# Squares of the attention heads summed during the attention, and an output phase without GpSimd whose blocks end one block later

## The chip, the cores and the metric

The kernel runs on one core of one Trainium2 chip. A core has TensorE (PE: matmuls, and PEld, their weight loads), VectorE (DVE), ScalarE (ACT), GpSimd (POOL), SyncE (SP, which issues transfers here), 16 DMA engines, the on-chip memory SBUF and the matmul accumulators in PSUM. The metric is the device time of one execution in microseconds, as the median of several.

## The reference, cut to what matters

One layer of a hybrid encoder over 4096 new tokens and 32 sample tokens, width 1024. A projection feeds a group of four differential-attention heads (values of 128) and a pooling group; both are gated, joined, multiplied by an output matrix, added to the residual, and normalised. The part that the change touches is the path from a head's output to the layer's output:

```
o = diff_attention(q, k, v)                       # per token and head: 128 values
o = rmsnorm(o, subln_g, 1e-5) * (1.0 - lam_init)  # root of the mean square of each head
a_out = o * silu(ga)
p_out = pool_mix(u) * silu(gp)
y = x + concat(a_out, p_out) @ w_out
y_out = rmsnorm(y, final_g, 1e-6)
```

## The kernel before

Work is cut into 32 blocks of 128 tokens and one block of 32 (the sample). Matmuls that need full precision are done as three products of a high and a low half (`mm3`, lines 112 to 114). Four phases follow one another on PE: the projection (`token_phase`), the gates and the pooling (`channel_phase`), the attention (`attention_phase`), and the output (`output_phase`).

The attention goes row by row; a row is one head and one block of queries, 128 rows in all. A row's scores (L616) are reduced to a maximum on DVE (L513), turned into exponentials on ACT (L522), joined on DVE (L554), transposed on PE (L560), copied on ACT (L563) and multiplied with the values on PE (L644). When the last value matmul of a row is done, DVE writes `ot`, the head's output, from the accumulator `av` (L649, two buffers), and SP stores it in `o_scr` (L650). One call of `step` puts at most one tile of scores, one transpose and one value product into the program. While work lasts, `step` also puts filler matmuls in between: the remaining channel work and `PoolPart`, the pooling half of the output product (`yp`, stored in `x_scr`), of which ten units are kept for the end.

The output phase takes the blocks in the order `LAST`. `heads_in` loads a block's head outputs and its gates into one tile (`on` and `gt`, shown as og), four blocks ahead, and works out the norm: a maximum (L908), a scale for very large values, four Squares on ACT (L916), nine small DVE operations on 4 columns, a root on ACT (L922) and a product on GpSimd (L929). `mixed` transposes the four heads on PE into the one PSUM tile with the tag tp (L935), multiplies them with the gate on DVE (L936), makes the high half on ACT (L938) and the low half on GpSimd (L939), and loads the residual from `x_scr` (L941). The main loop does 24 matmuls for a block, with `mixed` of the block after next between the two halves. `finish` adds the residual (L951), sums the squares (L952), works out the root (L954 to L957), scales (L960) and stores (L961). An engine carries out its instructions in order, SP its transfers too; the order on each engine is laid down by a planner before the run, close to the order of the program. Tiles with the tag m (og, residuals, exponentials) share 16 slots, and a transfer into a slot waits on SP until the slot is free.

Of the kernel before, what the change touches and what calls it, by code (L numbers as in the profile page):

```python
# [20 lines left out]
P = 128  # L21
# [47 lines left out]
def encoder(tc, a, o):  # L69
# [4 lines left out]
    with ExitStack() as es:  # L74
# [29 lines left out]
        def t_tile(shape, name):  # L104
            return tiny.tile(shape, F32, name=name)
# [388 lines left out]
        def attention_phase(first, filler, weights_in):  # L494
# [101 lines left out]
            class PromptRow(Row):  # L596
# [54 lines left out]

            class SampleRow(Row):

# [57 lines left out]
                def apply(self, g, x, n):  # L711
                    if self.av is None:
                        self.av = p1_tile("av", "av")
                    for i in range(n):
                        vc = s_tile([P, 512], name="vc")
                        if g == 0:
                            dma(vc, a["cv"][(x + i) * P:(x + i + 1) * P, :])
                            T.matmul(self.av, self.at[:, i], vc, start=x + i == 0, stop=False)
                        else:
                            dma(vc[:DEC].rearrange("t (h e) -> t h e", h=NH),  # L720
                                v_scr[:, :DEC, NB].rearrange("h t e -> t h e"))
                            T.matmul(self.av, self.at[:DEC, 0], vc[:DEC], start=False, stop=True)
                    if g == 1:
                        ot = tiny.tile([P, P], F32, name="ot", bufs=2)
                        for h in range(NH):
                            r = slice(h * DEC, (h + 1) * DEC)
                            V.tensor_scalar_mul(ot[r], self.av[r, h * P:(h + 1) * P], self.inv[r, 0:1])
                            dma(o_scr[SEQ:TOK, h * P:(h + 1) * P], ot[r])


            waiting, flight, clock, vclock = [], [], [0.0], [0.0]

            def step(tile=None):
# [66 lines left out]
            for ri, (h, qb) in enumerate(rows):  # L800
# [15 lines left out]
                elif 1 <= x <= 8:  # L816
# [8 lines left out]
            while waiting or flight:  # L825
                step()
                buffers(len(rows))

# [61 lines left out]


        def output_phase():
            wo, seq = [], LAST + [NB]
# [6 lines left out]
            def heads_in(b):  # L900
# [8 lines left out]
                small = t_tile([P, NH], "small")  # L909
                V.tensor_scalar(small[:m], mx[:m], BIG, None, op0=ALU.is_le)  # L910
                sg = t_tile([P, NH], "sg")
                V.tensor_scalar(sg[:m], small[:m], SHRINK, None, op0=ALU.max)
                sq = t_tile([P, NH], "sq")
                junk = s_tile([P, P], BF16, name="junk")
                for h in range(NH):
                    S.activation(junk[:m], on[:m, h], AF.Square, scale=sg[:m, h:h + 1], accum_out=sq[:m, h:h + 1])  # L916
                va = t_tile([P, NH], "va")
                V.tensor_scalar(va[:m], small[:m], 1e-5, None, op0=ALU.mult)
                V.scalar_tensor_tensor(va[:m], sq[:m], 1.0 / P, va[:m], op0=ALU.mult, op1=ALU.add)
                V.reciprocal(va[:m], va[:m])  # L920
                rr = t_tile([P, NH], "rr")
                S.activation(rr[:m], va[:m], AF.Sqrt)  # L922

                of = t_tile([P, NH], "of")
                V.scalar_tensor_tensor(of[:m], small[:m], 1.0, sq[:m], op0=ALU.subtract, op1=ALU.mult)
                V.tensor_scalar(of[:m], of[:m], -(2.0 ** -12), None, op0=ALU.is_gt)
                V.tensor_mul(rr[:m], rr[:m], of[:m])
                V.tensor_mul(rr[:m], rr[:m], sg[:m])
# [3 lines left out]
            def mixed(b, t0, m, on, gt):  # L932
# [9 lines left out]
                return b, t0, m, hl, xn  # L942

            def finish(blk, yp, fg):
                b, t0, m, hl, xn = blk
                last = b == seq[-1]
                ysq = t_tile([P, 2], "ysq")
                junk2 = s_tile([P, D], BF16, name="junk2")
                for n in range(2):
                    r = slice(n * 512, (n + 1) * 512)  # L950
                    V.tensor_add(xn[:m, r], yp[n][:m], xn[:m, r])  # L951
                    S.activation(junk2[:m, r], xn[:m, r], AF.Square, accum_out=ysq[:m, n:n + 1])  # L952
# [5 lines left out]
                out = o["y_prompt"][t0:t0 + m, :] if b < NB else o["y_sample"]  # L958
                for r in [slice(0, 512), slice(512, D)] if last else [slice(0, D)]:
                    V.scalar_tensor_tensor(xn[:m, r], xn[:m, r], yr[:m], fg[:m, r], op0=ALU.mult, op1=ALU.mult)  # L960
                    dma(out[:, r], xn[:m, r])  # L961

            def run():
                fg = m_tile([P, D], name="fg")
                dma(fg, a["final_g"])
                ahead = [heads_in(b) for b in seq[:4]]
                blks = []
                while part.left:
                    part.unit()
                    if part.left in (1, 3):  # L970
                        blks.append(mixed(*ahead.pop(0)))
                for x in range(NB + 1):
                    if x + 4 < NB + 1:
                        ahead.append(heads_in(seq[x + 4]))
                    b, t0, m, hl, xn = blk = blks.pop(0)
                    yp = p2_tile("yp")
                    yp = [yp[:, :512], p2_tile("yp")[:, :512] if b == seq[-1] else yp[:, 512:]]
                    for n in range(2):
                        for k in range(4):
                            out_half(yp[n], wo, hl, m, n, k)  # L980
                        if n == 0 and ahead:
                            blks.append(mixed(*ahead.pop(0)))
                    finish(blk, yp, fg)

            return weights_in, run

# [58 lines left out]
```

## Time and profile before

| | before |
|---|---|
| median of 3 runs | 2879.76 us (2876.3 to 2879.82) |
| the profiled execution | 2880.96 us, its span 2879.2 us |
| busy: PE, DVE, ACT, POOL | 2797.2, 1877.8, 1579.5, 361.1 us |
| share of the span: PE, DVE, ACT, POOL | 97%, 65%, 55%, 13% |
| mean granted clock of PE | 0.994 |
| moved by DMA | 348.52 MB, 121 GB/s |

The span runs from the first to the last instruction; the execution's own time is 1.76 us more. Busy shares are means over phases with different limits: the attention runs from about 1180 to 2640 us, the output phase from there to the end. A busy PE is not a PE at its peak, since matmuls overlap and their ends are modelled: matmuls of 512 columns that follow each other without a pause are listed with 0.39 us each, but start every 0.23 us.

### The profile page before, as it was taken

What the parts mean: (1) busy time and instruction counts of PE and PEld (TensorE: products, weight loads), DVE (VectorE), ACT (ScalarE), POOL (GpSimd) and SP (SyncE); (2) the same over time, 40 slices, a digit from 0 to 9 for tenths busy, and PEclk for the clock granted to TensorE, in tenths of its full rate; (3) what the DMA queues carried; (4) which work ended last, traced back from release to release, by engine and by line L of the source; (5) the groups of instructions that cost most, each with busy time, mean ns of one, the idle gap of its engine ahead of it and who ended that gap; (6) DMA issues with size and microseconds to landing.
All of it is one profiled execution on the core that took longest, in us unless ns stands there. A gap on an engine that the chain in (4) does not pass through costs nothing.

```text
span 2879.2 us, 44827 instructions
## 1 busy us (share of the span) xinstructions
PE 2797.2 (97%) x16637; PEld 2418.3 (84%) x16637; DVE 1877.8 (65%) x3721; ACT 1579.5 (55%) x3275; POOL 361.1 (13%) x577
## 2 busy tenths in 40 slices
PE   8999999999999999899999999999999999999998
PEld 7888888878888889788887888898888878888776
DVE  3221121265555555778877877887888888888897
ACT  4222222242222221577876777776787778887554
POOL 1111111010000011100001000011000110001332
PEclk9999999999999999999999999999999999999999
DMA  8555555652333334833336434356243342215773
GB/s 251 162 166 166 170 163 159 186 172 95 106 113 110 107 87 138 175 65 74 83 68 132 109 97 108 72 104 124 67 91 73 72 101 38 50 30 168 227 235 128
DMA packets 320012, 348.52 MB, mean 121 GB/s; under 512 B 26905, under 2 KB 250385, under 8 KB 319025
## 3 DMA queue, kind: packets, MB, share of 16 engines
q1 hardware_dynamic: 245184, 270.01, 30.2%
q0 software_dynamic: 74608, 75.64, 15.1%
q8 instruction: 131, 2.15, 0.3%
q14 instruction: 89, 0.72, 0.1%
HBM read 210.32 MB, written 135.26 MB: 120 GB/s over the span
## 4 chain that ended last, share of the span: by engine, by line
PE 83%; DVE 5%; DMA 4%; ACT 4%; issue 2%; SPq 1%; POOL 0%; DVEq 0%; ACTq 0%; POOLq 0%
PE sc L616 15%; PE av L644 13%; PE ps L114 12%; PE ps L112 12%; PE ps L113 12%; PE tp L560 7%; PE yp L112 3%; PE yp L113 3%; PE yp L114 3%; ACT p L522 2%; DMA o_scr<-ot 2%; DVE nm L513 2%; DVE p L554 1%; PE tp L253 1%; DMA wst<-w_in 1%
## 5 line engine op out<-in xcount | busy, mean ns | idle before, releaser
L513 DVE TENSOR_REDUCE nm<-sc 128x1 f32<-128x1024 f32 (+8 forms) x612 | 635.7, 1045 | 114.8 <-PE sc L616 109.0
L616 PE MATMUL sc<-kv,qt 128*128 128x512 f32 (+2 forms) x2304 | 667.4, 404 | 18.9 <-ACT p L522 13.9
L644 PE MATMUL av<-kv,at 128*128 128x128 f32 x4224 | 577.0, 276 | 12.8 <-DVE ot L649 12.5
L644 PEld LDWEIGHTS av<-kv,at 128*128 128x128 f32 x4224 | 549.8, 192 | 45.3 <-DVE ot L649 15.9
L616 PEld LDWEIGHTS sc<-kv,qt 128*128 128x128 f32 x2304 | 389.9, 191 | 91.7 <-ACT p L522 40.9
L522 ACT ACTIVATE p<-sc,nm 128x1024 f32<-128x1024 f32 (+7 forms) x386 | 359.9, 933 | 103.1 <-DVE nm L513 97.3
L563 ACT COPY at<-tp 128x512 f32<-128x512 f32 (+3 forms) x579 | 317.3, 548 | 174.0 <-PE tp L560 170.7
L112 PE MATMUL ps<-w,xh 128*128 128x512 f32 (+3 forms) x1056 | 357.5, 340 | 9.0 <-ACT w L146 8.4
L113 PE MATMUL ps<-w,xh 128*128 128x512 f32 (+3 forms) x1056 | 356.1, 338 | 0.7 <-DVE w L147 0.6
L114 PE MATMUL ps<-w,xl 128*128 128x512 f32 (+3 forms) x1056 | 355.9, 337 | 0.2 <-DVE xl L109 0.2
L554 DVE SCALAR_TENSOR_TENSOR p<-p,c 128x1024 f32<-128x1024 f32 (+5 forms) x322 | 344.2, 1080 | 2.5 <-issue 0.2
L560 PE MATMUL tp<-ident,p 128*128 128x128 f32 x2121 | 332.6, 275 | 2.3 <-ACT at L563 1.9
L112 PE MATMUL ps<-x,w 128*128 128x512 f32 (+2 forms) x864 | 319.0, 369 | 1.1 <-DVE u L386 1.1
L114 PE MATMUL ps<-x,w 128*128 128x512 f32 (+2 forms) x864 | 318.2, 368 | 0.0
L113 PE MATMUL ps<-x,w 128*128 128x512 f32 (+2 forms) x864 | 317.6, 368 | 0.0
L522 ACT ACTIVATE p<-sc,ref 128x1024 f32<-128x1024 f32 (+7 forms) x258 | 262.3, 1017 | 68.0 <-DVE ref L517 50.4
L560 PEld LDWEIGHTS tp<-ident,p 128*128 128x128 f32 x2121 | 250.8, 141 | 44.5 <-ACT at L563 17.9
L112 PE MATMUL yp<-wo,hl 128*128 128x512 f32 (+1 forms) x528 | 220.0, 417 | 5.7 <-DVE xn L881 4.9
L112 PEld LDWEIGHTS ps<-w,xh 128*128 128x128 f32 (+1 forms) x1056 | 198.0, 188 | 31.5 <-ACT w L146 8.9
L113 PEld LDWEIGHTS ps<-w,xh 128*128 128x128 f32 (+1 forms) x1056 | 198.5, 188 | 22.6 <-DVE w L147 1.8
L114 PEld LDWEIGHTS ps<-w,xl 128*128 128x128 f32 (+1 forms) x1056 | 198.3, 188 | 22.7 <-DVE xl L109 0.4
L114 PE MATMUL yp<-wo,hl 128*128 128x512 f32 (+1 forms) x528 | 210.0, 398 | 0.6 <-POOL hl L939 0.6
(158 smaller groups left out, 3501.3 us busy)
## 6 DMA issues: line engine op xcount, KB each, us to landing
xn<-xn SPq DMA_DIRECT2D x64, 512.0 KB, 3.9
qt<-q_scr POOLq DMA_DIRECT2D x128, 256.0 KB, 4.3
xt<-xT SPq DMA_DIRECT2D x32, 512.0 KB, 5.0
hl<-gp_scr POOLq DMA_DIRECT2D x32, 512.0 KB, 5.2
kv<-k_scr POOLq DMA_DIRECT2D x32, 512.0 KB, 9.0
x_scr<-xn SPq DMA_DIRECT2D x32, 512.0 KB, 4.7
xn<-x_scr SPq DMA_DIRECT2D x32, 512.0 KB, 4.2
y_prompt<-xn SPq DMA_DIRECT2D x32, 512.0 KB, 4.2
```

Of the source, the lines that this page charges most:

```text
L112: T.matmul(ps, lh, rh, start=first, stop=False)
L113: T.matmul(ps, lh, rl, start=False, stop=False)
L114: T.matmul(ps, ll, rh, start=False, stop=last)
L253: T.transpose(tp[:, h, :m], qk[:m, i * 512 + h * P:i * 512 + (h + 1) * P], ident[:m, :m])
L513: V.tensor_reduce(ref if self.ng == 1 and j else bias, sc, axis=AX.X, op=ALU.max, negate=True)
L522: S.activation(p[:, :w], sc, AF.Exp, bias=bias, accum_out=self.l[:, j, g:g + 1])
L554: V.scalar_tensor_tensor(p1[:, :w], p2[:, :w], self.c[:, g:g + 1], p1[:, :w], op0=ALU.mult, op1=ALU.add)
L560: T.transpose(tp[:blk.shape[1], i], blk, ident)
L563: S.copy(at[:r, :n], tp[:r, :n])
L616: T.matmul(sc[:, off:off + pw], qt[:, x, j, q0:q0 + P], keys[:, kk:kk + pw], start=x == 0, stop=x == 1)
L644: T.matmul(self.av[:, 0:P], self.at[:, i], self.value(kb), start=self.blk == 0, stop=self.blk == self.qb)
```

## The change

The sums of squares that the norm of the head outputs needs are taken by ACT during the attention, three steps after a row has ended, into one tile `sqs` for all blocks. For that, `ot` is clipped to plus and minus 2^64 on DVE, and has three buffers. The output phase works out the norms of 28 blocks at once, the last four in its twentieth block, and scales the heads by four Copies on ACT. The low half moves from GpSimd to DVE. In the main loop the residual is added and squared half by half, and the final scaling and the store of a block stand one block later. The sample's squares stay in the output phase.

```diff
-BIG = 2.0 ** 40
-SHRINK = 2.0 ** -70
+SHRINK = 2.0 ** -20
+CLIP = 2.0 ** 64
...
+        sqs = const.tile([P, NB + 1, NH], F32, name="sqs")
+        sink = const.tile([P, P], BF16, name="sink")
+
+        def square(out, src, m, x, h):
+            S.activation(out[:m], src, AF.Square, scale=SHRINK, accum_out=sqs[:m, x, h:h + 1])
...
-                        ot = tiny.tile([P, P], F32, name="ot", bufs=2)
-                        V.tensor_scalar_mul(ot, self.av[:, 0:P], self.inv[:, 0:1])
+                        ot = tiny.tile([P, P], F32, name="ot", bufs=3)
+
+                        V.tensor_scalar(ot, self.av[:, 0:P], self.inv[:, 0:1], CLIP, op0=ALU.mult, op1=ALU.min)
+                        V.tensor_scalar_max(ot, ot, -CLIP)
                         dma(o_scr[self.qb * P:(self.qb + 1) * P, self.h * P:(self.h + 1) * P], ot)
+                        squares.append([3, ot, LAST.index(self.qb), self.h])
...
             def step(tile=None):
 
+                for s in squares:
+                    s[0] -= 1
+                while squares and (squares[0][0] < 0 or not (waiting or flight)):
+                    _, ot, x, h = squares.pop(0)
+                    square(sink, ot, P, x, h)
...
+                dma(on[:m].rearrange("t h e -> t (h e)"), o_scr[t0:t0 + m, :])
                 dma(gt[:, :, :m], g_scr[:, :, t0:t0 + m].rearrange("e p t -> p e t"))
-                dma(on[:m].rearrange("t h e -> t (h e)"), o_scr[t0:t0 + m, :])
-                mx = t_tile([P, NH], "mx")
-                V.tensor_reduce(mx[:m], on[:m], axis=AX.X, op=ALU.max, apply_absolute_value=True)
...
-                G.tensor_mul(on[:m], on[:m], rr[:m].unsqueeze(2).to_broadcast([m, NH, P]))
-                return b, t0, m, on, gt
...
+            def norms(x0, x1, m=P):
+
+                sq, rr = sqs[:m, x0:x1], fgs[1][:m, x0:x1]
+                V.tensor_scalar(rr, sq, 2.0 ** 100, P * 1e-5 * SHRINK ** 2, op0=ALU.min, op1=ALU.add)
+                V.reciprocal(rr, rr)
+                S.activation(rr, rr, AF.Sqrt, scale=P * SHRINK ** 2)
+                V.scalar_tensor_tensor(rr, sq, 2.0 ** 128 * SHRINK ** 2, rr, op0=ALU.is_lt, op1=ALU.mult)
+
+            def scaled(blk):
+
+                x, t0, m, on, gt = blk
+                if x == NB:
+                    for h in range(NH):
+                        square(sink, on[:m, h], m, x, h)
+                    norms(x, x + 1, m)
                 for h in range(NH):
...
+                    S.activation(on[:m, h], on[:m, h], AF.Copy, scale=fgs[1][:m, x, h:h + 1])
...
-                G.tensor_sub(hl[:, 1, :, :m], gt[:, :, :m], hl[:, 0, :, :m])
...
+            def low(x, t0, m, hl, gt, xn):
+                V.tensor_sub(hl[:, 1, :, :m], gt[:, :, :m], hl[:, 0, :, :m])
...
+                for k in range(4):
+                    out_half(yp[0], wo, hl, m, 0, k)
+                half(blk, yp, 0, ysq)
+                if done:
+                    finish(*done)
+                if ahead:
+                    blks.append(mixed(*ahead.pop(0)))
+                    if ahead:
+                        scaled(ahead[0])
+                    low(*blks[-1])
+                for k in range(4):
+                    out_half(yp[1], wo, hl, m, 1, k)
+                half(blk, yp, 1, ysq)
+                done = root(blk, ysq)
+            finish(*done)
```

Here `half` is the add of the residual and the Square of one half of a block (L951, L952 of before), `root` the operations up to the root (L954 to L957), `finish` the scaling and the store (L960, L961).

## Rows read from the trace of the kernel before

**Rows 1.** Busy time by stretch: length, PE, PEld, DVE, ACT, POOL, clock, DMA share, GB/s
```profile
1180.00:2310.00 1130.00, 1103.89 (x7187) 968.63 (x7188) 901.26 (x1728) 845.85 (x1685) 110.94 (x251) 0.99 0.45 94
2310.00:2630.00 320.00, 308.49 (x2133) 271.82 (x2132) 274.89 (x548) 271.30 (x555) 21.77 (x53) 0.99 0.25 52
2655.00:2690.00 35.00, 35.00 (x168) 29.03 (x167) 30.14 (x88) 19.06 (x71) 13.14 (x10) 1.00 0.88 292
2733.38:2801.10 67.72, 61.02 (x281) 48.20 (x281) 66.69 (x171) 38.58 (x153) 25.94 (x20) 1.00 0.70 229
```

**Rows 2.** PE's timeline, output phase: start, duration, [idle before <- releaser]
```profile
2660.88 0.60 PE L935 MATMUL op<-ident,og 128*128 128x128 f32 x4
2666.79 0.60 PE L935 MATMUL op<-ident,og 128*128 128x128 f32 x4
...
2760.47 0.63 PE L935 MATMUL op<-ident,og 128*128 128x128 f32 x4 [0.68 <-issue]
...
2767.24 0.63 PE L935 MATMUL op<-ident,og 128*128 128x128 f32 x4 [0.67 <-issue]
...
2856.66 0.42 PE L935 MATMUL op<-ident,og 32*128 32x32 f32 x4 [1.89 <-issue]
```

**Rows 3.** Timeline of GpSimd and DVE ahead of the transposes at 2760.47 us
```profile
2758.17 1.04 POOL L929 TENSOR_TENSOR og<-og,rr 128x512 f32<-128x512 f32 x1 [2.25 <-DVE small L910]
2758.20 1.03 DVE L912 TENSOR_SCALAR sg<-small 128x4 f32<-128x4 f32 x1
...
2759.68 0.69 DVE L936 TENSOR_TENSOR og<-op,og 128x512 f32<-128x512 f32 x1
```

**Rows 4.** DVE's groups by line, 2733.38 to 2801.10 us: count | busy us, mean ns
```profile
L919 DVE SCALAR_TENSOR_TENSOR va<-sq,va 128x4 f32<-128x4 f32 x10 | 12.5, 1251 | 0.0
...
L936 DVE TENSOR_TENSOR og<-op,og 128x512 f32<-128x512 f32 x10 | 6.9, 691 | 0.0
L908 DVE TENSOR_REDUCE mx<-og 128x4 f32<-128x512 f32 x10 | 6.7, 672 | 0.0
```

**Rows 5.** Groups by line and shape, whole run, operations near the added ones
```profile
L916 ACT ACTIVATE junk<-og,sg 128x128 bf16<-128x128 f32 x128 | 50.3, 394 | 1.2
...
L549 ACT ACTIVATE p<-p,d 128x128 f32<-128x128 f32 x12 | 5.0, 414 | 0.0
...
L343 DVE TENSOR_SCALAR dg<-ident,rx 128x128 f32<-128x128 f32 x32 | 8.2, 281 | 4.5 <-PE bps L344 4.5
```

**Rows 6.** The end: busy time by stretch, and two matmuls of the timeline
```profile
2850.00:2879.00 29.00, 20.71 (x85) 14.34 (x84) 17.48 (x39) 8.85 (x28) 3.71 (x4) 0.91 0.25 95
...
2857.61 0.63 PE L113 MATMUL yp<-wo,hl 128*128 128x512 f32 x1
...
2860.49 0.39 PE L114 MATMUL yp<-wo,hl 128*128 128x512 f32 x1
```

**Rows 7.** PE's waits, 2640 to 2879 us: total us, times, longest
```profile
PE op L935 <- issue: 18.8, 23, 3.4
PE op L935 <- POOL og L929: 0.9, 1, 0.9
```

**Rows 8.** ACT's timeline around the end of the attention
```profile
2639.28 0.39 ACT L916 ACTIVATE junk<-og,sg 128x128 bf16<-128x128 f32 x1
...
2642.47 1.28 ACT L922 ACT_TABLE_LOAD   x1
```

**Rows 9.** Chain of waits by line, 1180 to 2310 us, then 2310 to 2630 us
```profile
by line: PE sc L616 29.7%; PE av L644 26.4%; PE tp L560 13.4%; PE yp L112 4.4%; PE yp L113 4.2%; PE yp L114 4.2%; DMA o_scr<-ot 3.6%; ACT p L522 2.5%; DVE nm L513 2.1%; DVE p L554 1.9%; issue 1.8%; DMA xn<-xn 0.9%; DVE xn L881 0.7%; DMA x_s
...
by line: PE sc L616 26.2%; PE av L644 26.0%; PE tp L560 14.3%; ACT p L522 10.7%; DVE nm L513 6.2%; DVE p L554 3.3%; ACT p L549 3.3%; DMA o_scr<-ot 3.1%; ACT at L563 2.7%; issue 2.1%; ACT d L524 0.9%; DVE ot L649 0.3%; DVE ref L517 0.3%; DVE
```

**Rows 10.** PE's waits, 1180 to 2630 us; and a piece of the chain
```profile
PE av L644 <- DVE ot L649: 12.3, 6, 5.8
...
1556.03 14.99 DMA o_scr<-ot
```

**Rows 11.** SP's waits, 2640 to 2879 us
```profile
SPq L941 <- DMA y_prompt<-xn: 80.1, 23, 5.8
```

More of the change, by code (lines that the diff above doesn't have):

```diff
@@ L723, in apply @@
                     if g == 1:
-                        ot = tiny.tile([P, P], F32, name="ot", bufs=2)
+                        ot = tiny.tile([P, P], F32, name="ot", bufs=3)
                         for h in range(NH):
                             r = slice(h * DEC, (h + 1) * DEC)
-                            V.tensor_scalar_mul(ot[r], self.av[r, h * P:(h + 1) * P], self.inv[r, 0:1])
+                            V.tensor_scalar(ot[r], self.av[r, h * P:(h + 1) * P], self.inv[r, 0:1], CLIP, op0=ALU.mult, op1=ALU.min)
+                            V.tensor_scalar_max(ot[r], ot[r], -CLIP)
                             dma(o_scr[SEQ:TOK, h * P:(h + 1) * P], ot[r])
             waiting, flight, clock, vclock = [], [], [0.0], [0.0]
+            squares = []
             def step(tile=None):
+                for s in squares:
[3 more added lines that the diff above has]
+                    square(sink, ot, P, x, h)
                 due = waiting and (tile is None or waiting[0][0] <= clock[0])
@@ L824, in attention_phase @@
                         finish_row(sample)
-            while waiting or flight:
+            while waiting or flight or squares:
                 step()
@@ L892, in output_phase @@
         def output_phase():
-            wo, seq = [], LAST + [NB]
+            wo, seq, fgs = [], LAST + [NB], [None]
             def weights_in(slots):
@@ L898, in weights_in, with heads_in @@
                 wo.extend(out_parts(tiles))
-            def heads_in(b):
+            def heads_in(x):
+                b = seq[x]
                 t0, m = b * P, (P if b < NB else DEC)
@@ L911, in heads_in @@
[L911 to L914, printed above, removed]
-                for h in range(NH):
-                    S.activation(junk[:m], on[:m, h], AF.Square, scale=sg[:m, h:h + 1], accum_out=sq[:m, h:h + 1])
-                va = t_tile([P, NH], "va")
-                V.tensor_scalar(va[:m], small[:m], 1e-5, None, op0=ALU.mult)
@@ L919, in heads_in @@
[L919 to L927, printed above, removed]
@@ L928, in heads_in @@
[L928 to L932 removed]
+                return x, t0, m, on, gt
+            def norms(x0, x1, m=P):
[4 more added lines that the diff above has]
+                V.scalar_tensor_tensor(rr, sq, 2.0 ** 128 * SHRINK ** 2, rr, op0=ALU.is_lt, op1=ALU.mult)
@@ L933, in mixed @@
+            def scaled(blk):
[4 more added lines that the diff above has]
+                    norms(x, x + 1, m)
+                for h in range(NH):
+                    S.activation(on[:m, h], on[:m, h], AF.Copy, scale=fgs[1][:m, x, h:h + 1])
+            def mixed(x, t0, m, on, gt):
                 op = p1_tile("tp", "op").rearrange("p (h t) -> p h t", h=NH)
@@ L938, in mixed, with half, root @@
                 S.copy(hl[:, 0, :, :m], gt[:, :, :m])
-                G.tensor_sub(hl[:, 1, :, :m], gt[:, :, :m], hl[:, 0, :, :m])
                 xn = m_tile([P, D], name="xn")
                 dma(xn[:m], x_scr[t0:t0 + m, :])
[L942 to L952, printed above, removed]
+                return x, t0, m, hl, gt, xn
+            def low(x, t0, m, hl, gt, xn):
+                V.tensor_sub(hl[:, 1, :, :m], gt[:, :, :m], hl[:, 0, :, :m])
+            def half(blk, yp, n, ysq):
+                x, t0, m, hl, gt, xn = blk
+                r = slice(n * 512, (n + 1) * 512)
+                V.tensor_add(xn[:m, r], yp[n][:m], xn[:m, r])
+                junk = s_tile([P, 512], BF16, name="junk2")
+                S.activation(junk[:m], xn[:m, r], AF.Square, accum_out=ysq[:m, n:n + 1])
+            def root(blk, ysq):
+                m = blk[2]
                 yr = t_tile([P, 1], "yr")
@@ L957, in finish @@
                 S.activation(yr[:m], yr[:m], AF.Sqrt)
-                out = o["y_prompt"][t0:t0 + m, :] if b < NB else o["y_sample"]
-                for r in [slice(0, 512), slice(512, D)] if last else [slice(0, D)]:
-                    V.scalar_tensor_tensor(xn[:m, r], xn[:m, r], yr[:m], fg[:m, r], op0=ALU.mult, op1=ALU.mult)
+                return blk, yr
+            def finish(blk, yr):
+                x, t0, m, hl, gt, xn = blk
+                out = o["y_prompt"][t0:t0 + m, :] if x < NB else o["y_sample"]
+                for r in [slice(0, 512), slice(512, D)] if x == NB else [slice(0, D)]:
+                    V.scalar_tensor_tensor(xn[:m, r], xn[:m, r], yr[:m], fgs[0][:m, r], op0=ALU.mult, op1=ALU.mult)
                     dma(out[:, r], xn[:m, r])
             def run():
-                fg = m_tile([P, D], name="fg")
+                fg = fgs[0] = m_tile([P, D], name="fg")
+                fgs.append(s_tile([P, NB + 1, NH], name="rrs"))
                 dma(fg, a["final_g"])
-                ahead = [heads_in(b) for b in seq[:4]]
-                blks = []
+                ahead = [heads_in(x) for x in range(4)]
+                norms(0, NB - 4)
+                for blk in ahead[:3]:
+                    scaled(blk)
+                blks, done = [], None
                 while part.left:
@@ L971, in run @@
                         blks.append(mixed(*ahead.pop(0)))
+                        low(*blks[-1])
                 for x in range(NB + 1):
                     if x + 4 < NB + 1:
-                        ahead.append(heads_in(seq[x + 4]))
-                    b, t0, m, hl, xn = blk = blks.pop(0)
-                    yp = p2_tile("yp")
[L977 to L983, printed above, removed]
+                        ahead.append(heads_in(x + 4))
+                    if x == 20:
+                        norms(NB - 4, NB)
+                    blk = blks.pop(0)
+                    m, hl = blk[2:4]
+                    yp = p2_tile("yp")
+                    yp = [yp[:, :512], p2_tile("yp")[:, :512] if x == NB else yp[:, 512:]]
+                    ysq = t_tile([P, 2], "ysq")
+                    for k in range(4):
[7 more added lines that the diff above has]
+                            scaled(ahead[0])
+                        low(*blks[-1])
+                    for k in range(4):
[3 more added lines that the diff above has]
+                finish(*done)
             return weights_in, run
```

2 lines of the change are left out of this document (removed).

## The prediction

> **What bounds the kernel now.** First the busy time of each engine by stretch [rows 1]. In the attention (1180 to 2630 us) PE is busy for 1103.89 of 1130 us and 308.49 of 320; in the last 320 us DVE and ACT are not far behind (274.89 and 271.30), since no filler matmuls are left there. In the output phase the picture turns: over ten blocks (2733.38 to 2801.10 us) DVE is busy for 66.69 of 67.72 us and PE for only 61.02, although PE had run without a pause from 2655 to 2690 us at the same clock.
>
> Then PE's timeline [rows 2]. The transposes of the head outputs mark one block each. Early on they are 5.91 us apart (2660.88, 2666.79) with PE never idle, so 5.91 us is the floor: 24 matmuls and four transposes. Later they are 6.77 us apart (2760.47, 2767.24), with an idle 0.68 or 0.67 us ahead of them. The releaser is "issue", so the profile names nothing. The code does: the transposes write the one PSUM tile of tag tp, and DVE's product L936 must have read the block before out of it. That product starts at 2759.68 and lasts 0.69 us [rows 3], to 2760.37; the transposes start at 2760.47. PE waits for DVE's queue.
>
> Why is DVE full? A four-element operation (L912) takes 1.03 us and ends at 2759.23, together with the GpSimd product L929 that runs from 2758.17 for 1.04 us [rows 3]. So the small operation stands still while GpSimd works. L919, also of four elements, takes 1.251 us on the mean [rows 4], at the time of the other GpSimd operation.
>
> **What the change takes out of a block, and what it adds.** DVE spends 6.67 us per block (66.69/10, rows 1). Removed: L912 (1.03, rows 3), L919 (1.251) and L908 (0.672) [rows 4], and seven more tiny ones that I leave uncounted. Added: the low half, a subtraction of 512 elements that GpSimd did; nearest row L936 of the same shape, 0.691 us [rows 4]. That gives at most 6.67 - 1.03 - 1.25 - 0.67 + 0.69 = 4.41 us, below 5.91. ACT spends 38.58/10 = 3.86 us [rows 1]; four Squares go (0.394 each) and four scaled Copies come (0.414 for such a Copy) [rows 5], so at most 3.94 us. GpSimd does nothing. PE's work stays, so PE is the only engine that needs 5.91 us.
>
> The order inside a block also frees PE: the product that empties tp stands behind one add and one final scaling of the block before, some 2 us after the transposes, and the next transposes come 5.9 us after. The final scaling a block later needs no wait for its root.
>
> Sum for the output phase: from the fourth transposes at 2660.88 to the last at 2856.66 are 195.78 us in 29 blocks; at the floor 29 x 5.91 = 171.4. **Gain 24.4 us.** Of it 18.8 us stand as idle time ahead of the transposes [rows 7]; the rest lies in matmuls that run on at a lower clock or with an empty pipeline after such a pause. After the last transposes the granted clock is 0.91 over the stretch, and seven matmuls take 2860.49 - 2857.61 = 2.88 us [rows 6] where they take 7 x 0.227 = 1.6 at full clock (0.227: the floor less 0.47 for the transposes, over 24). PE had been idle for 1.89 us just before. Without that pause about **1.3 us** comes back. At the start of the phase PE waits 0.9 us for the first GpSimd product [rows 7]. That goes, but a new chain takes its place: the batched norms of 28 blocks (two DVE operations, table load and root on ACT, one DVE operation), then four Copies. The table load of 1.28 us [rows 8] is there before too. I take nothing; the ends are a gain of 1 and a loss of 3 (a table load and four Copies in sequence on an idle PE). For the sample block, whose own squares and norms run in series on ACT and DVE, about 4 Squares and 4 Copies, 3.2 us plus handovers, within one block of 5.9: I take **1 us** of loss, ends 0 and 3.
>
> **What is added to the attention.** 128 rows get a Square on ACT (0.394, rows 5; its read of the sum overlaps the next) and a max on DVE. A max of 128x128 from SBUF is not in the trace; the nearest is L343, a scalar operation of that shape, 0.281 us [rows 5]. The min rides in the existing operation. The Square is put three steps after its row, so ot should be there; behind it in ACT's queue stand the exponentials and the copies that PE's value matmuls wait for.
> How much of this reaches the end? The chain of waits [rows 9] gives shares. In 1180 to 2310 us, ACT's exponentials have 2.5% and DVE 2.1 + 1.9 + 0.7 = 4.7%; 94 rows x (0.39 x 0.025 + 0.28 x 0.047) = 2.2 us. In 2310 to 2630 us ACT has 10.7 + 3.3 + 2.7 + 0.9 = 17.6% and DVE 6.2 + 3.3 = 9.5%, more with small items; 34 rows x (0.39 x 0.176 + 0.28 x 0.10) = 3.3 us. **Loss 5.5 us.** Bounds: nothing, if PE stays saturated, and 34 x 0.67 = 23 us if every added operation of the stretch without filler is in series.
>
> The third buffer of ot takes away a wait. PE's value matmuls wait 12.3 us, in six places, for the DVE operation that writes ot [rows 10]; the worst of them because the transfer of an earlier ot took 14.99 us to land, and with two buffers the third product must wait for it. With three it has a whole row more. **Gain 10 us**, ends 0 and 12. It is less if the Square holds the buffer longer, but rows end some nine microseconds apart (34 in 320 us), and three steps are a few.
>
> **A rule that speaks against it.** Squares of the old output phase run at 2639.28 us, directly behind the attention's copies, and the only table load of that stretch comes at 2642.47, for the root [rows 8]: so a Square runs under the table of the exponential. The Trainium skill (ScalarE: Activation LUTs, section "Table sets: the hidden batching unit") says that functions come in named sets and a switch costs about 2.7 us, and it does not name Square among those that every set has. By that, an exponential behind each Square would need two loads: by the row's 1.28 us, 128 x 2 x 1.28 = 328 us, so 3209; by the page's figure twice that. The row excludes it but for a changed table choice; I leave 1 in 100.
>
> **Sum.** -24.4 - 1.3 + 1 + 5.5 - 10 = -29.2 us. The profiled execution took 2880.96 us (span 2879.2), 1.2 above the median of 2879.76. So 2851.8 for that execution and **2851** against the median.
>
> **Rivals.**
> (a) The output phase leaves DVE and meets SP's queue. SP waits 80.1 us in 23 places for a finished block's store before it can load the next residual into that slot [rows 11], and behind that load stand the head loads. At the floor the phase must move its bytes in 5.91 instead of 6.77 us: 229 GB/s at a DMA share of 0.70 becomes 262 GB/s at 0.80. For it: stores now come a block later, and hold a slot longer. Against it: from 2655 to 2690 us the DMA moved 292 GB/s at a share of 0.88 with PE never idle [rows 1], and the loads are three to four blocks ahead. If half the gain is lost: 2863. Chance 0.20.
> (b) The other side: the Square stands at the head of ACT's queue before its ot is written, and the exponentials wait. The rest gains 24.4 + 1.3 + 10 - 1 = 34.7 us, so it decides from 34.7/128 = 0.27 us of lost PE time per row. At a full Square per row (0.39) it is 50 us: 2895. For it: ACT is busy for 271 of 320 us in the last stretch. Against: three steps of delay, and PE has filler work for 94 of the 128 rows. Chance 0.09 of reaching the break-even.
> (c) The pauses of PE are not DVE's queue, and GpSimd does not hold DVE up: then the output phase keeps its 6.77 us, and only ot's buffer and the attention's load remain, -10 + 5.5, hence 2875; with no help from the buffer, no change. The common end of L912 and L929 speaks against it. Chance 0.05.
> The tables' rival has 0.01, the forecast 0.65.
>
> **How the numbers follow.** The forecast's own range comes from its bounds: all gains at their ends and no loss, -24.4 - 1.3 - 1 - 12 = -39, hence 2841; attention at 15 instead of 5.5, 2860. To hold 8 in 10 the range must take in most of (a): up to 2868, and down to 2841. A change under 0.2% (5.8 us) cannot be told from none here. Faster: forecast, (a) and half of (c), about 0.88; same: rest of (c) and the part of (b) near its break-even, 0.04; slower: (b) and the tables, 0.08.
>
> **What will show it.** Right: transposes 5.9 us apart from the first to the last, no "issue" ahead of them, DVE near 4.4 us a block, small DVE operations at 0.16 us; no wait of value matmuls for ot; table loads as before. Wrong: a period above 6.2 us with ACT or DVE waiting for transfers of og or xn is (a); new idle time of PE behind exponentials between 2310 and 2630 us, with ACT waiting for ot, is (b). A second cause for error: the planner places all instructions anew, and a new stall in the attention could take ten microseconds either way.

## The result, and the profile after

The changed kernel takes **2850.65 us** (median of 4 runs, 2848.12 to 2851.88) against 2879.79 us: a ratio of 0.9898, with a 95% interval of 0.9881 to 0.9915. The forecast was 2851. That the sum came out to the microsecond is luck: two of its terms, the blocks of the output phase and the third buffer, were off by 8 and about 10 us in opposite directions, so the point of what follows is where the time came from. The profiled execution took 2851.88 us, its span 2850.1 us, at a mean granted clock of 0.996 (0.994 before).

The page's busy times, after:

```profile
PE 2791.5 (98%) x16637; PEld 2413.9 (85%) x16637; DVE 1832.5 (64%) x3565; ACT 1601.2 (56%) x3377; POOL 277.3 (10%) x511
```

The stretches of rows 1, after. As there: length, PE, PEld, DVE, ACT, POOL, clock, DMA share, GB/s. The last row is a stretch of 80 us of the output phase.

```profile
1180.00:2310.00 1130.00, 1112.27 (x7268) 976.62 (x7269) 924.37 (x1843) 879.95 (x1892) 114.23 (x256) 1.00 0.46 95
...
2310.00:2630.00 320.00, 307.37 (x2122) 272.03 (x2121) 275.20 (x574) 278.00 (x611) 18.91 (x48) 0.98 0.26 53
...
2733.38:2801.10 67.72, 67.72 (x314) 53.78 (x313) 48.20 (x93) 38.38 (x120) 0.00 (x0) 1.00 0.77 251
...
2720.00:2800.00 80.00, 79.90 (x369) 63.17 (x368) 56.60 (x109) 45.54 (x141) 0.00 (x0) 1.00 0.80 260
```

In the stretch of 67.72 us PE and DVE have changed places: PE is busy all of it, DVE for 48.20 us (66.69 before [rows 1]), and GpSimd does nothing. PE's timeline, after: the last value matmul of the attention, then transposes of the output phase (the fourth, two late ones, the last).

```profile
2629.06 1.73 PE L650 MATMUL av<-kv,at 128*128 128x128 f32 x14
...
2649.47 0.60 PE L947 MATMUL op<-ident,og 128*128 128x128 f32 x4
...
2774.27 0.60 PE L947 MATMUL op<-ident,og 128*128 128x128 f32 x4
...
2780.34 0.60 PE L947 MATMUL op<-ident,og 128*128 128x128 f32 x4
...
2828.96 0.43 PE L947 MATMUL op<-ident,og 32*128 32x32 f32 x4
```

The idle time ahead of the transposes is gone. But they are 2780.34 - 2774.27 = 6.07 us apart, not 5.91. And the attention ends at 2629.06 + 1.73 = 2630.8 us; before, the same row read

```profile
2638.30 1.73 PE L644 MATMUL av<-kv,at 128*128 128x128 f32 x14
```

and ended at 2640.0. So of the 29.1 us between the two spans, 9.2 were gained by the end of the attention, and 18.5 between there and the last transposes: the start of the phase (last value matmul to fourth transposes, 20.9 to 18.7) gave 2.2, the 29 blocks (195.78 to 2828.96 - 2649.47 = 179.5) gave 16.3. The remaining 1.4 came behind them. The prediction had 4.5 for the attention and 24.4 for the blocks.

The 9.2 us lie behind the first head output, which DVE writes at the same time in both traces, before and after:

```profile
1188.99 0.33 DVE L649 TENSOR_SCALAR ot<-av,inv 128x128 f32<-128x128 f32 x1
```

```profile
1188.99 0.33 DVE L656 TENSOR_SCALAR ot<-av,inv 128x128 f32<-128x128 f32 x1
```

Ahead of that, PE stands still once, in the change for 6.02 us up to 1182.47: a filler's add (L897) waits for a load.

```profile
1182.47 0.80 PE L112 MATMUL yp<-wo,hl 128*128 128x512 f32 x1 [6.02 <-DVE xn L897]
```

Before, this wait is 3.6 us long, and in the traces of the other kernels it runs from nothing to 4.6. The first Square starts at 1190.54 us, so the wait is not the Squares' doing, and lengths of the attention are better compared from the first head output on.

PE's waits, after: in the attention (1180 to 2630 us), then in the output phase (2640 to 2830 us). Total us, times, longest.

```profile
PE sc L622 <- DMA kv<-k_scr: 5.3, 1, 5.3
...
PE av L650 <- DVE ot L656: 1.3, 1, 1.3
...
PE yp L112 <- DVE xn L962: 2.6, 3, 1.3
```

The wait for `ot` fell from 12.3 [rows 10] to 1.3 us. A single wait for keys of 5.3 us stands out. In the output phase a wait is new: matmuls for an add of the residual (L962). The weight loads, which run ahead of the matmuls, show it in each block:

```profile
2775.21 0.19 PEld L112 LDWEIGHTS yp<-wo,hl 128*128 128x128 f32 x1 [0.31 <-DVE xn L962]
```

### The profile page after: what moved, and what is told of

Read it like the earlier page. It is cut to its first block, busy times and chain, and to the rows that moved or that the text cites. A ratio compares the mean times of both kernels' runs of the same rounds, so it can differ in the third digit from the quotient of the medians.

```text
span 2850.1 us, 44682 instructions
## 1 busy us (share of the span) xinstructions
PE 2791.5 (98%) x16637; PEld 2413.9 (85%) x16637; DVE 1832.5 (64%) x3565; ACT 1601.2 (56%) x3377; POOL 277.3 (10%) x511
```

## The experiments

Theory at the outset: GpSimd's two operations held DVE up, and freeing DVE gives the output phase's gain; the third buffer of `ot` gives a gain of its own in the attention, and the Squares take some of it back. Rivals: that the batched norms or the later end of a block did the work, and that the Squares cost nothing or far more. Each kernel is compared with the kernel before on the same chip; medians are given with the ratio and its interval. The medians of the kernel before in the four groups of runs lie from 2878.62 to 2880.34 us, so a difference between medians of two groups is uncertain by a microsecond or two besides the spread of the runs.

**Two buffers of ot in the changed kernel.**

```diff
-                        ot = tiny.tile([P, P], F32, name="ot", bufs=3)
+                        ot = tiny.tile([P, P], F32, name="ot", bufs=2)
```

> The changed kernel with two buffers of ot in place of three. If the third buffer is what shortened the attention (the last value matmul ended at 2630.5 us in place of 2639.8), the value matmuls wait for ot again, 10 us or more, and the time is 2860 us or a little above, since a row's Square now holds one of only two buffers. Rival: the attention got shorter because the planner laid it out anew, and the buffer is worth nothing: 2851 us, within 3.

Measured: 2869.84 us, 0.9963 (0.9949 to 0.9977). PE's waits in the attention:

```profile
PE av L650 <- DVE ot L656: 11.8, 4, 5.5
```

The wait is back, and 19 us with it, nearly twice the 10 that I gave this term.

**Three buffers of ot in the kernel before**, and nothing else.

```diff
-                        ot = tiny.tile([P, P], F32, name="ot", bufs=2)
+                        ot = tiny.tile([P, P], F32, name="ot", bufs=3)
```

> The kernel before with three buffers of ot and nothing else. If the waits for the transfer of ot are what the buffer takes away, PE's 12.3 us of waits for ot go and the time is 2868 to 2871 us. Rival: PE loses the same time a little later to another wait (the keys' transfer, DVE's queue), and the time stays at 2878 to 2881 us.

Measured: 2859.11 us, 0.9928 (0.9913 to 0.9942), a gain of 21 us where the forecast was 9 to 12; the wait is

```profile
PE av L644 <- DVE ot L649: 3.4, 5, 1.3
```

That is 8.9 us less waiting for a gain of 21. The granted clock holds much of the rest. The kernel before, around its longest wait for `ot` (5.81 us, up to 1571.5), in the columns of rows 1, and PE's timeline there:

```profile
1565.70:1571.50 5.80, 0.02 (x1) 0.00 (x0) 0.38 (x2) 0.89 (x2) 0.00 (x0) 0.88 1.43 227
1571.50:1575.00 3.50, 3.47 (x14) 3.38 (x15) 1.26 (x2) 1.66 (x3) 0.00 (x0) 0.50 0.10 26
1575.00:1580.00 5.00, 5.00 (x26) 4.28 (x26) 3.07 (x6) 1.56 (x5) 0.00 (x0) 0.81 0.04 13
```

```profile
1571.53 2.07 PE L644 MATMUL av<-kv,at 128*128 128x128 f32 x8 [5.81 <-DVE ot L649]
...
1578.38 1.05 PE L644 MATMUL av<-kv,at 128*128 128x128 f32 x8
```

Behind the pause PE runs at 0.50, the lower of the two levels (1.2 of 2.4 GHz), and the same eight matmuls take 2.07 us and later 1.05. The stretches behind this one pause lose 3.5 x 0.50 + 5 x 0.19 = 2.7 us on top of the 5.81. Over the whole span the mean clock rises from 0.994 to 0.997, some 0.003 x 2879 = 9 us, uncertain by about 3 from the rounding. With the 8.9 us of waits that makes about 18 of the 21. The split is an estimate: a mean over the whole span also holds what other pauses cost.

**No GpSimd operation in the output phase of the kernel before.** The norms stay as they were, block by block.

```diff
-                G.tensor_mul(on[:m], on[:m], rr[:m].unsqueeze(2).to_broadcast([m, NH, P]))
+                for h in range(NH):
+                    S.activation(on[:m, h], on[:m, h], AF.Copy, scale=rr[:m, h:h + 1])
...
-                G.tensor_sub(hl[:, 1, :, :m], gt[:, :, :m], hl[:, 0, :, :m])
+                V.tensor_sub(hl[:, 1, :, :m], gt[:, :, :m], hl[:, 0, :, :m])
```

> The kernel before with its two GpSimd operations of the output phase moved: the product to four scaled Copies on ACT, the low half to DVE. Norm, attention and the end of a block stay as before. If GpSimd's use of the port that DVE shares is what filled DVE, DVE falls to 6.67 - 0.87 - 1.1 + 0.69 = 5.4 us a block, below PE's 5.91; ACT rises to 3.86 + 1.66 = 5.5. The period becomes 6.0 to 6.1 us and the time 2857 to 2862 us. Rival: DVE is full of its own work, and the period stays above 6.7 us: 2878 to 2884 us; what helps in the change is then the removal of the maximum and the small operations.

Measured: 2863.18 us, 0.9943 (0.9928 to 0.9958). From the last value matmul to the last transposes the trace has 198.4 us, as in the changed kernel (216.9 before). The small DVE operations of rows 3 and 4, in the groups by line from 2733 to 2801 us:

```profile
L912 DVE TENSOR_SCALAR sg<-small 128x4 f32<-128x4 f32 x11 | 1.8, 168 | 0.1
...
L919 DVE SCALAR_TENSOR_TENSOR va<-sq,va 128x4 f32<-128x4 f32 x11 | 1.7, 156 | 0.1
```

They take 0.16 us where they took 1.03 and 1.25. All nine are still there; only GpSimd's two operations have moved. So moving its two operations is by itself worth what the whole edit of the output phase gave, and the batched norms are not needed for it.

**Both in the kernel before:** the two edits above together.

> The kernel before with three buffers of ot, and with its GpSimd operations of the output phase on ACT and DVE. Alone they gave 21 and 17 us. If they are independent (attention and output phase), 2842 us, and the rest of the change (Squares in the attention, batched norms, the end of a block later) costs 8 us. Rival: they share the same gain, 2850 us or more.

Measured: 2842.6 us, 0.987 (0.9855 to 0.9885). The gains add (21 + 17 = 38, measured 37.7), and this kernel, without a Square in the attention, is 8 us faster than the change.

**The low half back on GpSimd** in the changed kernel.

```diff
-                V.tensor_sub(hl[:, 1, :, :m], gt[:, :, :m], hl[:, 0, :, :m])
+                G.tensor_sub(hl[:, 1, :, :m], gt[:, :, :m], hl[:, 0, :, :m])
```

> The changed kernel with the low half back on GpSimd, and nothing else there. If GpSimd holds DVE up, DVE operations that run beside it last 0.5 to 1.2 us longer, but DVE stays below 5.3 us a block, so PE still sets the period: 2849 to 2854 us, with lengthened operations in the trace. Rival: the contention alone decides, and the period goes back towards 6.7 us: 2865 us or more.

Measured: 2863.62 us, 0.994 (0.9923 to 0.9956), 13 us lost by taking an operation off DVE. The forecast that DVE's spare time would absorb it (2849 to 2854) failed. Stretch of 2720 to 2800 us, then DVE's and GpSimd's timelines, then the group of the final scaling by line:

```profile
2720.00:2800.00 80.00, 74.20 (x334) 58.44 (x333) 47.38 (x83) 38.74 (x121) 15.47 (x12) 0.98 0.72 231
```

```profile
2726.22 2.38 DVE L979 SCALAR_TENSOR_TENSOR xn<-xn,yr,fg 128x1024 f32<-128x1024 f32 x1 [0.79 <-ACT yr L972]
...
2730.94 1.28 DVE L979 SCALAR_TENSOR_TENSOR xn<-xn,yr,fg 128x1024 f32<-128x1024 f32 x1 [0.41 <-ACT yr L972]
```

```profile
2726.22 1.29 POOL L956 TENSOR_TENSOR hl<-og,hl 128x512 fp32r<-128x512 f32 x1 [3.96 <-ACT yr L972]
```

```profile
L979 DVE SCALAR_TENSOR_TENSOR xn<-xn,yr,fg 128x1024 f32<-128x1024 f32 x12 | 22.0, 1831 | 7.9 <-ACT yr L972 7.9
```

The scaling that starts with GpSimd's subtraction lasts 2.38 us, the one alone 1.28: it loses 1.10 of the 1.29 us that GpSimd works. The Trainium skill (SBUF — State Buffer, section "Who interferes with whom") says that a DVE instruction with two inputs in SBUF contends with a GpSimd instruction that reads SBUF; `xn` and `fg` are two such inputs, and the trace agrees. It also shows that DVE need not be full for this to cost: it is busy for 47.38 of 80 us. The stretched operation delays the next add of a residual, and PE's matmuls wait for that add six times in this stretch, 6.6 us in all:

```profile
PE yp L112 <- DVE xn L962: 6.6, 6, 1.9
```

**The end of a block in the same block** again, in the changed kernel.

```diff
-                    if done:
-                        finish(*done)
...
-                    done = root(blk, ysq)
-                finish(*done)
+                    finish(*root(blk, ysq))
```

> The changed kernel with the final scaling and the store in the block itself, as before, in place of one block later. If the delay spares DVE the wait for the root, DVE now stands for some 1.9 us a block behind ACT's Square and root, comes to 6.3 us a block and PE waits for it: period 6.1 to 6.4, 2853 to 2862 us. Rival: the planner puts other work into the gap, and the delay is worth nothing: 2848 to 2852 us.

Measured: 2850.7 us, 0.9902 (0.9881 to 0.9922). DVE's groups by line, 2720 to 2800 us, here and then in the changed kernel:

```profile
L979 DVE SCALAR_TENSOR_TENSOR xn<-xn,yr,fg 128x1024 f32<-128x1024 f32 x13 | 16.6, 1275 | 0.0
```

```profile
L979 DVE SCALAR_TENSOR_TENSOR xn<-xn,yr,fg 128x1024 f32<-128x1024 f32 x14 | 17.9, 1276 | 0.0
```

No idle time ahead of the scaling in either. Ending a block one block later is worth nothing that these runs show; the interval is some 6 us wide to either side.

**A PSUM tile for each half** of a block's output, in the changed kernel.

```diff
-                    yp = [yp[:, :512], p2_tile("yp")[:, :512] if x == NB else yp[:, 512:]]
+                    yp = [yp[:, :512], p2_tile("yp")[:, :512]]
```

> The changed kernel with a PSUM tile of its own for each half of the output product, as its last block has. After the change the blocks are 6.07 us apart, not 5.91, and the weight load of the second half waits for DVE's add of the first half. If that wait comes from the two halves sharing a tile, the period falls to 5.91 to 5.95, and with 30 blocks and the few longer ones 4 to 8 us come back: 2843 to 2847 us. Rival: the 0.15 us are the price of the order of the matmuls, or the third tile is missed elsewhere: 2850 us or more.

Measured: 2843.26 us, 0.9871 (0.9856 to 0.9886), 7 us faster than the change. PE's timeline has the transposes 5.93 us apart,

```profile
2704.10 0.60 PE L947 MATMUL op<-ident,og 128*128 128x128 f32 x4
2710.03 0.60 PE L947 MATMUL op<-ident,og 128*128 128x128 f32 x4
```

and the weight loads' wait for the add is gone. In the change, DVE adds the residual to the first half while the second half of the same PSUM tile is due to be written, and the second half's first matmul is made to wait for that add. The 29 blocks take 174.4 us (179.5 in the change, 171.4 at the floor).

**No Squares in the attention.** `sqs` is filled with ones, so the norms of the 32 prompt blocks are left out; the clipping stays.

```diff
-                    square(sink, ot, P, x, h)
...
+        V.memset(sqs, 1.0)
```

> The changed kernel without the 128 Squares of the attention; the sums of squares of the prompt blocks are left at 1, so this part of the norm is left out. If the Squares cost what the shares of the chain say (0.39 us each, at 2.5% and 17.6%), 3 us come back: 2846 to 2849 us. Rival: a Square holds up ACT's queue in front of the exponentials, and costs most of its 0.39 us: 30 to 50 us come back, 2800 to 2820 us. Third: nothing comes back, 2851.

Measured: 2847.17 us, 0.9887 (0.987 to 0.9903): 3.5 us less than the change, within the spread of the runs (2841.45 to 2853.08 here), and inside the forecast.

**Each Square twice.**

```diff
                     square(sink, ot, P, x, h)
+                    square(sink, ot, P, x, h)
```

> The changed kernel with each Square of the attention done twice. If the Squares cost what the shares of the chain say, another 3 us: 2852 to 2856 us. If they cost the 9 us that the attention is longer with them: 2858 to 2862. If each stands in ACT's way in full (128 x 0.39 = 50 us): 2895 to 2905. If the longer attention is the fault of one late load of keys at the start of the last head, and not of ACT's time: 2850 to 2852.

Measured: 2855.22 us, 0.9916 (0.99 to 0.9932): 4.6 us for 128 more Squares, 0.036 us each.

**Squares over one column** of 128, so that the operation stays and loses a part of its length; the sums lack 127 of 128 values.

```diff
-                    square(sink, ot, P, x, h)
+                    square(sink[:, 0:1], ot[:, 0:1], P, x, h)
```

> The changed kernel with the Squares of the attention over one column in place of 128, so that they keep their places and waits and lose two thirds of their time; the sums of squares are those of one column, so the norm is left out in part. If the attention is longer with Squares because of their time on ACT, most of the 9 us come back (attention 1444 to 1447 us, wait for keys near 2320 us below 3 us). If it is the order that comes with them, nothing comes back: attention 1449 to 1456 us, the wait for keys 5 to 6.6 us, 2848 to 2852 us in all.

Measured: 2842.29 us, 0.9872 (0.9857 to 0.9886), 8.4 us less than the change. What a Square costs ACT, by line and shape in the attention: the change, then this kernel.

```profile
L167 ACT ACTIVATE sink<-ot 128x128 bf16<-128x128 f32 x127 | 40.0, 315 | 4.1 <-DVE ot L657 4.0
L167 ACT ACTIVATION_READ_ACCUMULATOR sink<-ot 128x1 f32 x127 | 25.5, 201 | 0.0
```

```profile
L167 ACT ACTIVATE sink<-ot 128x1 bf16<-128x1 f32 x128 | 26.9, 210 | 5.3 <-DVE ot L657 5.1
```

Only 13 us of ACT's time went, and 8.4 came back in the medians, more than the 3.5 of leaving the Squares out. So this is not the price of ACT's time alone; the planner lays the program out anew for each kernel, and the traced execution, 2847.91 us, is the slowest of the four. One place shows part of the gain, the change of heads near 2320 us, where PE waits for new keys: PE's timeline of the change, then of this kernel.

```profile
2322.23 5.15 PE L622 MATMUL sc<-kv,qt 128*128 128x512 f32 x12 [5.33 <-DMA kv<-k_scr]
```

```profile
2317.80 2.88 PE L622 MATMUL sc<-kv,qt 128*128 128x512 f32 x12 [2.72 <-DMA kv<-k_scr]
```

The stretches there, in the columns of rows 1: the change, then this kernel.

```profile
2320.00:2325.00 5.00, 2.77 (x7) 2.22 (x8) 0.54 (x2) 0.00 (x0) 0.00 (x0) 0.53 0.35 89
2325.00:2330.00 5.00, 3.47 (x11) 2.25 (x9) 4.39 (x9) 3.53 (x6) 0.00 (x0) 0.79 0.01 2
```

```profile
2318.00:2325.00 7.00, 4.21 (x18) 3.03 (x18) 5.34 (x12) 4.13 (x8) 0.00 (x0) 1.00 0.00 1
2325.00:2330.00 5.00, 3.46 (x17) 2.23 (x16) 4.90 (x8) 5.00 (x9) 0.10 (x1) 1.00 0.00 0
```

The wait is 2.6 us shorter and the clock does not fall. From the end of that pause to the end of the attention it is 308.6 us in the change and 306.5 here. In all six kernels with whole Squares in the attention the pause at this place is 5.0 to 6.6 us; in the others it is 2.6 to 3.2.

Why do the keys come later? The transfers at this place show it: the loads of the keys (POOL L586, two of them) and one load of a filler's residual (SP L886), in the change, then in this kernel.

```profile
2307.91 1.19 POOL L586 DMA_DIRECT2D kv<-k_scr  x2 [1.10 <-PE av L650]
```

```profile
2309.89 0.33 SPq L886 DMA_DIRECT2D xn<-xn  x1
```

```profile
2306.49 1.18 POOL L586 DMA_DIRECT2D kv<-k_scr  x2 [1.11 <-PE av L650]
```

```profile
2298.94 0.33 SPq L886 DMA_DIRECT2D xn<-xn  x1
```

In the six kernels with whole Squares the residual is issued 1 to 3 us behind the keys, and the later keys take 12.7 to 14.3 us to land; in the other eight it has landed before the keys are issued, and they take 9.5 to 10.4. So the order of transfers on SP, which changed with the edit, goes with the late keys in all 14 traces. No run changes that order alone, so the cause is not shown by experiment. It also means that the kernel with one column differs from the change in more than the length of its Squares.

**Squares back in the output phase**, one block ahead of the Copies, with own PSUM tiles.

```diff
+            def squared(blk):
+                x, t0, m, on, gt = blk
+                for h in range(NH):
+                    square(sink, on[:m, h], m, x, h)
+                norms(x, x + 1, m)
...
+                        if len(ahead) > 1:
+                            squared(ahead[1])
```

> The changed kernel with a PSUM tile for each half of the output product, and the Squares of all blocks back in the output phase, one block ahead of the scaling, each block with norms of its own. ACT then has 3.9 + 4 x 0.39 + 0.2 = 5.7 us a block and DVE 4.4 + 0.5 = 4.9. If the Squares cost the attention some 9 us (1452 us with them, 1443 without, as means of the kernels run so far) and the output phase has room for them, the attention falls to 1440 to 1446 us, the output phase stays at 193 to 198, and the time is 2832 to 2840 us. Rival: ACT becomes the limit of the output phase, as in the kernel before with GpSimd's work moved: 201 us or more, and 2842 us or above.

Measured: 2847.07 us, 0.9894 (0.9877 to 0.9912). The forecast was missed, and the time is the rival's. The attention is as long as without Squares (from the first head output to the last value matmul 1437.2 us; 1435.3 without Squares, 1441.5 in the change), but the output phase takes 201.5 us instead of 193.2 with own PSUM tiles. ACT, the rival's limit, is busy for 56.96 of 80 us (2720 to 2800), so it is not full. From about the thirteenth block on, every other block takes 6.9 to 7.6 us.

**The same, with two PSUM tiles for the transposes in turn.**

```diff
-                op = p1_tile("tp", "op").rearrange("p (h t) -> p h t", h=NH)
+                op = p1_tile("tp" if x % 2 else "av", "op").rearrange("p (h t) -> p h t", h=NH)
```

> The kernel with the Squares back in the output phase and PSUM tiles for each half, and now two PSUM tiles for the transposes, in turn (the second is the one of the attention's value products, free by then). If the 7 us blocks of its second half come from the transposes waiting for DVE's product out of the one tile, they go, the output phase falls from 201 to 194 to 197 us, and the time is 2838 to 2843 us. Rival: the blocks are late because ACT or the loads of the heads are, and another wait takes the place: 2845 to 2849 us.

Measured: 2852.45 us, 0.9912 (0.9899 to 0.9926), no better; the forecast of 2838 to 2843 was missed. All engines' waits from 2720 to 2820 us in this kernel:

```profile
ACT sink L167 <- DMA og<-o_scr: 16.9, 11, 2.6
...
DVE rrs L928 <- ACT sink L167: 6.8, 6, 2.4
PE yp L112 <- DVE rrs L928: 6.7, 6, 1.4
```

So the transposes' tile was not what held it up. By these waits, the Squares stand at the head of ACT's queue until a block's heads have landed, and what follows on ACT and DVE, and in the end PE, waits with them. That earlier heads would cure it was not tried.

## Why the prediction was right, point by point

**PE waits for DVE, and GpSimd holds DVE up: right.** Without GpSimd the small operations take 0.16 us, and the output phase gains 18.5 us with nothing else changed; with one GpSimd operation put back, the changed kernel loses 13 us. Rival (c) falls. DVE's busy time, foreseen as at most 4.41 us a block, is 56.60 x 6.07 / 80 = 4.29, ACT's 3.46 (foreseen at most 3.94). A detail was wrong: I took a full queue as the condition. With DVE at 59% one stretched operation was enough.

**Output term, -24.4: mis-sized.** The blocks gave 16.3. The step that failed is "transposes 5.9 us apart from the first to the last": I looked for waits at the transposes only and did not cost the half-by-half add, which makes the second half's matmuls wait for the first half's add (0.15 us a block, 4.4 in 29 blocks; own PSUM tiles brought 7 us in the medians). A few longer blocks (up to 7.47 us), most of them in the first half of the phase, are the rest, some 3.6 us. The start of the phase, taken as 0, gave 2.2, beyond its end of 1; the end, -1.3, gave 1.4.

**"The final scaling a block later needs no wait for its root": no effect.** The same with the end in its own block: 2850.7.

**Third buffer, -10, ends 0 and 12: mis-sized.** It measured 21 in the kernel before and 19 in the change. The mechanism was right (the wait went from 12.3 to 3.4 and 1.3 us), but I priced it by the waits alone; by the estimate above, PE's return at the lower clock about doubles it, and the end of 12 was too near. I had counted that loss at the end of the output phase [rows 6] and not here.

**Squares and max in the attention, +5.5: near in size, wrong in place.** Leaving the Squares out gave 3.5 us, doubling them cost 4.6, cutting them to one column gave 8.4. By the pages of the profile, ACT is busy for 1601.2 us with the Squares and 1565.2 without, 0.28 a Square, where I priced 0.39 (its two records of 0.315 and 0.201 us overlap each other and their neighbours); the max (L657) took

```profile
L657 DVE TENSOR_SCALAR ot<-ot 128x128 f32<-128x128 f32 x127 | 28.1, 222 | 0.5
```

0.222 us where I priced 0.281. Rival (b), the Square waiting at the head of ACT's queue, would need 0.27 us a row; ACT waits 4.0 us there in all (the group above), 0.03 a row, and 128 more Squares cost 0.036 each.

Where the time went shows in the timelines, from the first head output to the start of the last value matmul, cut at the pause for the last head's keys. All nine kernels have three buffers of `ot`; they differ in the output phase too, and in the planner's order.

| us | up to the pause | the pause | behind it |
|---|---|---|---|
| no max, no Squares (2 kernels) | 1122.0, 1122.7 | 2.8, 2.7 | 308.2, 308.4 |
| max alone (3) | 1124.1 to 1125.9 | 2.6 to 3.2 | 308.0 to 309.7 |
| max and Squares (4, the change among them) | 1127.3 to 1128.9 | 5.0 to 6.6 | 308.1 to 308.3 |

On the means the Squares cost 5 us and the max 3. But the prediction put 3.3 of its 5.5 us into the stretch behind 2310 us, where no filler work is left, and behind the pause neither the Squares nor the max cost anything in these traces. The loss of both, 8 us in these traces, lies ahead of the pause (5.5 us, where I had 2.2) and in the pause itself (2.8 us, the late keys, which the sum did not have). That the total comes near 5.5 is in part luck.

**Table loads: excluded.** As foreseen, there are six, each of 1.283 us, before and after. ACT's groups by line, after, the one of the norms:

```profile
L931 ACT ACT_TABLE_LOAD x1 | 1.3, 1283 | 0.0
```

Were Square in another set than the exponential, hundreds would stand here; a Square switches nothing in this trace.

**Rival (a), SP's queue: not at this period, or only mildly.** The DMA share rose to 0.80 (0.83 with the first blocks) and PE stayed at 79.90 of 80 us. But the heads do land late: ACT's Copies wait 8.2 us for them from 2720 to 2800 us, hidden behind PE. From 2640 to 2720 us they wait 13.4 us, and PE is busy for 77.42 of the 80; whether the longer blocks there come from these waits was not tried. In the two kernels with Squares in the output phase the same lateness came to the surface.

**The sum.** Attention 9.2 for 4.5, output and tail 19.9 for 24.7: the errors cancel, by luck. By the medians of the experiments, 21 + 17 us of gains less the 8 by which the kernel before with both edits is faster give the 29. In the traces those 8 lie in the attention (1433.0 us from the first head output in that kernel, 1441.5 in the change); its output phase is even 3 us longer (201.6 for 198.4).

What stays open: whether another order of transfers would bring the keys early in spite of the Squares, and what makes the 5.5 us ahead of the pause. Single traces also mislead by their start. In the kernel before with three buffers the last value matmul starts 19.5 us earlier than before (2620.3 for 2639.8 us), in the change 9.3 (2630.5), a difference of 10 us; 2.5 of them lie ahead of the first head output (1186.5 for 1189.0), and 7.7 are left for the Squares, the max and what the planner moved, as the medians give.

## What to carry to other kernels

Price a wait of PE by its length and by the clock behind it: here the two were about equal by the estimate, 8.9 and 9 us. Compare attention or phase lengths from an event that the edit can't have moved, not from the start of the trace. Look at which transfers an edit brings together: the load that PE needs next came 3 us later beside another. When two engines contend, look for the one long instruction that is stretched and who waits for it, not only at busy shares; and a part of a PSUM tile that is read while another part is due to be written wants a tile of its own. Test the parts of a bundled change alone: two of them (three buffers, no GpSimd) made a kernel 8 us faster than the whole, 2842.6 us, and one line more in the change itself (own PSUM tiles) comes to 2843.3.

## What was not expected of the hardware

The granted clock behind a pause does not follow from the length of the pause alone. Behind 2.72 us without matmuls, and a shorter pause after it, it stayed at 1.00 in the kernel with one-column Squares (above); in the kernel before, at the same place in the program and behind pauses of the same two lengths, but with 4 matmuls between them in place of 12, PE's timeline and the stretch behind are

```profile
2330.08 1.17 PE L616 MATMUL sc<-kv,qt 128*128 128x512 f32 x4 [2.72 <-DMA kv<-k_scr]
2332.66 3.57 PE L616 MATMUL sc<-kv,qt 128*128 128x512 f32 x8 [1.42 <-ACT p L522]
```

```profile
2332.00:2337.00 5.00, 4.12 (x9) 3.01 (x10) 4.01 (x11) 3.52 (x8) 0.00 (x0) 0.50 0.00 0
```

so a pause of that size can cost nothing or some 2 us more.
